# Ring tiles at multiples of 2048 bytes, and GpSimd's elementwise work on VectorE, in a hybrid decoder trunk

## The chip, the cores and the metric

One core of a Trainium2 chip runs the whole kernel. The metric is device microseconds of one execution; the runs shown give a median, and one further execution was profiled.

## The reference

One decoder layer on an input of 1024 tokens by 1024 channels, all in float32. The input is normalised, one wide projection (1024 x 10008) feeds four mixers, each mixer's result is projected back to 1024 channels, weighted by a sigmoid gate from the input, summed, passed through an output projection and added to the input. A SwiGLU feed-forward network and a final norm follow.

```python
xn = rmsnorm(h, norm_mix_w); proj = xn @ w_in
ya = hgrn2_branch(...); yb = ssd_branch(...); yc = gla_branch(...); yd = rglru_branch(...)
branch_out = einsum('blnw,nwd->blnd', stack([ya, yb, yc, yd]), w_branch)
merged = sum(sigmoid(mg) * branch_out, over the four)
h = h + merged @ w_out
xn = rmsnorm(h, norm_ffn_w)
h = h + (silu(xn @ w_gate) * (xn @ w_up)) @ w_ffn_out
return rmsnorm(h, norm_f_w)
```

The branch names: `ya` is HGRN2 and `yc` is GLA (both chunkwise gated linear attention), `yb` is the Mamba-2 SSD, `yd` is the RG-LRU.

## The kernel before, in words

**Split products.** A float32 product is made from three faster float32r matmuls. Every operand is split into a high part h (a rounded copy) and a low part l = raw - h, and the product is wh·ah + wh·al + wl·ah (`mm3`, L197 to 205; `mm3_tm`, L310 to 316; the feed-forward loops at L1105 to 1108 and L1201 to 1203). So each weight tile that arrives by DMA in `wr` costs a copy on ScalarE (L150) and a subtraction (L151). In the mixers `parts` (L148) does both, the subtraction on GpSimd (`G`). In the feed-forward network the same subtraction is written out on VectorE (`V`), at L1026, L1042, L1050, L1159 and L1168.

**Tiles.** All SBUF tiles of size come from one pool, `cp`. Rings of it are: `s` (26 slots of 128 x 1024), `wr`, `wh` and `wl` (two buffers each of 128 x 1024; raw weight, high, low), `t` (four of 128 x 512) and `x` (32 halves of 128 x 512, `half`). The pool gives a tag its place at the first tile taken of it, one behind the other, each tile padded to 32 bytes per partition. The pool begins 16512 bytes into a partition, 128 more than a multiple of 2048. Before the first slot come `prm0` (64 bytes), `prm` (448), `cst` (1536), `gtr` (1024) and `msk` (1024), 4096 in all. So the rings `s`, `wr` and `t` lie 128 bytes behind multiples of 2048. Then the 4-byte tiles `tiny` and `one` take 32 bytes each (L181 and L183), and `wh`, `wl` and `x`, whose first tiles are taken later, lie 192 bytes behind them. Operands of matmuls are columns of these tiles at multiples of 512 bytes, so an operand in `s` stands at 0 modulo 128 and one in `wh`, `wl` or `x` at 64.

**Stages.** In the order of time: load, norm and transposes into `x` halves (to about 40 us); RG-LRU (`conv` L403, gates L429, scans L458); then `merge(3)`; HGRN2 `attention` per head (L483), with the next head's projections between; `merge(0)`; GLA attention; the SSD's convolutions; `merge(2)` with one SSD `chunk` (L815) inside each of its steps; the SSD's gated norm (L892 to 915); eight gates, and the last branch (L930); the output projection (L1071); the feed-forward input (`ffn_in`) from about 1465 us and output (`tile_block`) from about 1895 us.

**`merge(b, y)`** (L390) runs over eight column tiles. Each step projects a gate (48 matmuls of 512 columns, `gate` L364) and a branch (24 matmuls, `branch` L376). VectorE multiplies gate and branch out of PSUM (L380), and the step adds into `merged` (L384, on GpSimd for three of the branches; the first has nothing to add to, the last one, at L930, is already on VectorE).

**What orders the work.** The tile framework orders the instructions of all engines ahead of time by priority and its own durations and puts in the semaphores; each engine then works through its own list in order. `tc.high_priority()` draws weight loads and their splits forward. DMAs of weights are issued by SyncE as the two `wr` buffers come free, that is after L150 and L151 have read them; L151 writes a `wl` buffer as soon as TensorE has done with the tile before the last (L205).

```python
def parts(h, l, raw):
    i = A.copy(h, raw)
    G.tensor_sub(l, raw, f32(h))
    return i
```

Of the kernel before, what the change touches and what calls it, by code (L numbers as in the profile page):

```python
# [30 lines left out]
F32 = mybir.dt.float32  # L31
F32R = mybir.dt.float32r
I32 = mybir.dt.int32
U8 = mybir.dt.uint8
# [4 lines left out]
P = 128  # L39
T = 1024  # L40
D = 1024
NT = T // P
KD = D // P
BW = 512
# [27 lines left out]
def trunk(ctx: ExitStack, tc: tile.TileContext, x, w_in, w_branch, w_out, w_fin, w_fout, prm_d, gw_d, lw_d,  # L72
          nfw_d, snw_d, cst_d, msk_d, out):
    nc = tc.nc
    V, A, G, TE = nc.vector, nc.scalar, nc.gpsimd, nc.tensor
    mult, add, sub, mx, mn = ALU.mult, ALU.add, ALU.subtract, ALU.max, ALU.min

    cp = ctx.enter_context(tc.tile_pool(name="cp", bufs=1))
# [37 lines left out]
    def f32(t):  # L116
        return t.bitcast(F32)
# [3 lines left out]
    prm = cp.tile([P, NPRM], F32, name="prm")  # L121
    cst = cp.tile([P, 3 * P], F32, name="cst")
    gtr = cp.tile([P, 2, P], F32R, name="gtr")
    msk = cp.tile([P, 2, 8, 64], U8, name="msk")

    ident, tri = cst[:, 0:P], (cst[:, P:2 * P], cst[:, 2 * P:3 * P])

# [20 lines left out]
    def parts(h, l, raw):  # L148

        i = A.copy(h, raw)  # L150
        G.tensor_sub(l, raw, f32(h))  # L151
        return i

    def load_w(src, nk, raw=None):
# [11 lines left out]
    for t in range(NT):  # L166
# [5 lines left out]
        if t % 4 == 3:  # L172
            c = C_LX + t // 4 * P
# [4 lines left out]
    nc.sync.dma_start(gt, cst_d[:, 3 * P:5 * P])  # L178
    mskf = slot()
    nc.sync.dma_start(mskf, msk_d)  # L180
    tiny = cp.tile([P, 1], F32, name="tiny")  # L181
    V.memset(tiny, 2.0 ** -115)
    one = cp.tile([P, 1], F32, name="one")  # L183
    V.memset(one, 1.0)

    def hs(hf):
        return slice(hf * H, (hf + 1) * H)
# [9 lines left out]
    def mm3(p, w, act):  # L197

        wh, wl = w
        n = len(act)  # L200
        for k, (ah, al) in enumerate(act):
            TE.matmul(p, lhsT=wh[k], rhs=ah, start=k == 0, stop=False)  # L202
            TE.matmul(p, lhsT=wh[k], rhs=al, start=False, stop=False)  # L203
        for k, (ah, al) in enumerate(act):
            TE.matmul(p, lhsT=wl[k], rhs=ah, start=False, stop=k == n - 1)  # L205

    def cut(w, nk, at=0):
        return [[a[:, k, at:at + P] for k in range(nk)] for a in w]
# [57 lines left out]
    for hf in range(2):  # L266
        norm_x(hf)
        if hf == 0:
            wlx.append(load_w(None, KD, rlx[0]))
        xn[hf] = split_fm(xt[hf * 4:hf * 4 + 4], "nmix", allbank)  # L270
        if hf == 0:
            wlx.append(load_w(None, KD, rlx[1]))
            for i in range(2):
                first[i] = dense_bank()
                mm3(first[i], cut(wlx[i], KD), xn[0])
    tc.keep_in_program_order(G.tensor_copy(gtr.rearrange("p a m -> p (a m)"), gt))
    tc.keep_in_program_order(G.tensor_copy(msk.rearrange("p a l m -> p (a l m)"), mskf))
    slot.free(mskf)
# [97 lines left out]
    def branch(b, dm, act, g, eng):  # L376

        ps = dense_fm(cut(wbr[b, dm // 2], 4, dm % 2 * P), act)
        for hf in range(2):
            V.scalar_tensor_tensor(g[:, hs(hf)], g[:, hs(hf)], 1.0, ps[hf], op0=add, op1=mult)  # L380
        if merged[dm] is None:
            merged[dm] = g
        else:
            eng.tensor_add(merged[dm], merged[dm], g)  # L384
            slot.free(g)

    def as_act(y):
        return [[(h[:, hs(hf)], l[:, hs(hf)]) for h, l in y] for hf in range(2)]

    def merge(b, y, also=None):  # L390

        for dm in range(KD):
            if also:
                also(dm)
            g = gate(b, dm)
            if dm % 2 == 0:
                load_br(b, dm)
            branch(b, dm, as_act(y), g, G)
        for h, l in y:
            slot.free(h, l)  # L400

# [51 lines left out]
    for i in range(4):  # L453
        j = A.activation(th[i], th[i], AF.Sqrt, bias=tiny)
# [5 lines left out]
    for i in range(4):  # L460
# [3 lines left out]
        g = act_slot(ps, AF.Gelu_apprx_tanh)  # L464
# [284 lines left out]
    NH = 8  # L749
# [31 lines left out]
    for ab in range(2):  # L781
# [4 lines left out]
            TE.matmul(pp, lhsT=gtr[:, ab, :], rhs=dahv[:, cols], start=True, stop=False)  # L786
            TE.matmul(pp, lhsT=gtr[:, ab, :], rhs=dalv[:, cols], start=False, stop=pp is after)
        TE.matmul(whole, lhsT=tri[ab], rhs=dav[:, cols], start=False, stop=True)
    ex = cp.tile([P, 3, NT, NH], F32, name="ex")
    A.activation(ex, p[:, 0:192].rearrange("p (i c h) -> p i c h", i=3, c=NT), AF.Exp)  # L790
    eg = cp.tile([P, NT, 4], F32, name="eg")
    V.tensor_copy(eg[0:64], ex[0:64, 2, :, 0:4])
    V.tensor_copy(eg[64:P], ex[64:P, 2, :, 4:8])
    bt = slot()
# [20 lines left out]
    def chunk(c):  # L815
        ab, at = c % 2, place(c)
        cs = slice(at * P, (at + 1) * P)
        xd = tmp()
        xdv = xd.rearrange("p (h q) -> p h q", h=NH)
        Xr = Xv[at // 2][:, at % 2, :]  # L820
        Xc = Xr.rearrange("p (h q) -> p h q", h=NH)
        V.tensor_tensor(xdv, Xc, dt[:, at, :].unsqueeze(2).broadcast_to(hb), op=mult)
        yp = sbank()
        for g in range(2):
            gs = slice(g * 64, (g + 1) * 64)
            cb = tbank()
            TE.matmul(cb[:, 0:P], lhsT=bt_f[gs, cs], rhs=ct[gs, cs], start=True, stop=True)
            cbm = cbm2()
            V.tensor_mul(cbm, cb[:, 0:P], tri[ab])

            lp = tbank()
            for i, part in enumerate((dah, dal)):
                td = tmp(F32R)
                V.tensor_tensor(quad(td), tri[ab].unsqueeze(1).broadcast_to([P, 4, P]),
                                  f32(part)[:, at, g * 4:(g + 1) * 4].unsqueeze(2).broadcast_to([P, 4, P]), op=mult)
                TE.matmul(lp, lhsT=gtr[:, ab, :], rhs=td, start=i == 0, stop=i == 1)
            dl = tmp()
            A.activation(dl, lp, AF.Exp)
            V.tensor_tensor(quad(dl), quad(dl), cbm.unsqueeze(1).broadcast_to([P, 4, P]), op=mult)
            for h in range(4):  # L840
                hh = g * 4 + h
                TE.matmul(yp[:, hh * 64:(hh + 1) * 64], lhsT=dl[:, h * P:(h + 1) * P], rhs=xdv[:, hh, :],
                          start=True, stop=True)
        V.tensor_tensor(Xc, Xc, pv("dsk", 0, 8).unsqueeze(2).broadcast_to(hb), op=mult)
        V.tensor_add(Xr, Xr, yp)
        if c:
            yt = tmp()
            for g in range(2):
                gs = slice(g * 64, (g + 1) * 64)
                yo = sbank()[:, 0:256]  # L850
                TE.matmul(yo, lhsT=ct[gs, cs], rhs=S[gs, c % 4, :], start=True, stop=True)
                V.tensor_tensor(yt[:, g * 256:(g + 1) * 256].rearrange("p (h q) -> p h q", h=4),
                                yo.rearrange("p (h q) -> p h q", h=4),
                                ex[:, 0, at, g * 4:(g + 1) * 4].unsqueeze(2).broadcast_to([P, 4, 64]), op=mult)
            G.tensor_add(Xr, Xr, yt)
        if c < NT - 1:
            V.tensor_tensor(xdv, xdv, ex[:, 1, at, :].unsqueeze(2).broadcast_to(hb), op=mult)
            up = tbank()
            for g in range(2):
                gs = slice(g * 64, (g + 1) * 64)  # L860
                TE.matmul(up[gs, 0:256], lhsT=btv[:, at, gs], rhs=xd[:, g * 256:(g + 1) * 256], start=True, stop=True)
            Sn = S[:, (c + 1) % 4, :]
            if c:
                V.tensor_tensor(Sn.rearrange("p (h q) -> p h q", h=4),
                                S[:, c % 4, :].rearrange("p (h q) -> p h q", h=4),
                                eg[:, at, :].unsqueeze(2).broadcast_to([P, 4, 64]), op=mult)
                V.tensor_add(Sn, Sn, up[:, 0:256])
            else:
                V.tensor_copy(Sn, up[:, 0:256])
# [14 lines left out]
    zz = [slot() for _ in range(4)]  # L884
# [7 lines left out]
    for c in range(NT):  # L892
        j, hf = c // 2, c // 4
        if c % 4 == 0:
            yb[hf] = [(slot(F32R), slot(F32R)) for _ in range(2)]
        Xr = Xv[j][:, c % 2, :]
        G.tensor_mul(Xr, Xr, zz[j][:, c % 2 * BW:(c % 2 + 1) * BW])
        sq = tmp()
        ss = sm.tile([P, 2], F32, name="ss2", tag="s2")
        for g in range(2):  # L900
            A.activation(sq[:, g * 256:(g + 1) * 256], Xr[:, g * 256:(g + 1) * 256], AF.Square, accum_out=ss[:, g:g + 1])
        r = rstd_of(ss, 2, 1.0 / 256)
        for g in range(2):
            gs = slice(g * 256, (g + 1) * 256)
            V.scalar_tensor_tensor(Xr[:, gs], Xr[:, gs], r[:, g:g + 1], snb[:, gs], op0=mult, op1=mult)
        p = tbank()
        for k in range(4):
            TE.transpose(p[:, k * P:(k + 1) * P], Xr[:, k * P:(k + 1) * P], ident)
        for kp in range(2):
            h, l = (a.rearrange("p (k t) -> p k t", k=2)[:, :, c % 4 * P:(c % 4 + 1) * P] for a in yb[hf][kp])  # L910
            pk = p[:, kp * 256:(kp + 1) * 256].rearrange("p (k t) -> p k t", k=2)
            A.copy(h, pk)
            V.tensor_sub(l, pk, f32(h))
        if c % 2:
            slot.free(X[j], zz[j])
# [11 lines left out]
    for dm in range(KD):  # L927
# [3 lines left out]
        for hf in range(2):  # L931
            h, l = half(F32R), half(F32R)
# [273 lines left out]
    for hf in range(2):  # L1206
# [11 lines left out]
        for t in range(4):  # L1218
            for j in range(NFF - LATE, NFF):
                tile_block(hf, t, j)  # L1220
            y, sq = slot(), slot()
# [81 lines left out]
```

## Time and profile before

| | us |
|---|---|
| median of 3 runs (2155.83 to 2160.21) | 2156.05 |
| the profiled execution, its own time | 2143.17 |
| span of the profiled execution | 2140.2 |
| TensorE busy | 2052.1 |
| VectorE busy | 974.3 |
| ScalarE busy | 634.0 |
| GpSimd busy | 328.1 |

In the profile PE is TensorE's matmuls, DVE is VectorE, ACT is ScalarE and POOL is GpSimd. L151 is line 151 of the kernel. A row's `[1.32 <-DVE t L834]` is the idle time of the engine ahead of the instruction and the instruction whose end released it. `pd<-x,wh` names the tiles that an instruction writes and reads, without buffer numbers; of a matmul's two operands one is the stationary (the weights held in the array, 128 columns) and one the moving one. Durations of matmuls overlap, so their pace is read from start to start. A granted clock of 1.00 is 2.4 GHz and 0.50 is 1.2 GHz.

### The profile page before, as it was taken

How to read it: one execution, taken by the hardware profiler on the slowest of the kernel's cores; microseconds unless marked ns; L12 is line 12 of the kernel's file. 1: busy time of each engine (PE TensorE's matmuls, PEld its weight loads, DVE VectorE, ACT ScalarE, POOL GpSimd, SP SyncE). 2: the span in 40 equal slices, each digit the busy share in tenths (PEclk: the TensorE clock that was granted, in tenths of full speed). 3: DMA queues.
4: the chain of work that ended last, by engine and by line, in shares of the span. 5: the costliest groups of instructions: out<-in, count | busy, mean ns of one | idle time of the engine just before them, and what ended most of it. 6: DMA issues, size and time to landing. Idle time of an engine off the chain costs nothing.

```text
span 2140.2 us, 24073 instructions
## 1 busy us (share of the span) xinstructions
PE 2052.1 (96%) x9892; PEld 1678.6 (78%) x9892; DVE 974.3 (46%) x1594; ACT 634.0 (30%) x943; POOL 328.1 (15%) x154
## 2 busy tenths in 40 slices
PE   6989999999999999989999899999999999999998
PEld 5679887889888777866668888776888888888886
DVE  6460005655110366556442504448666555554532
ACT  5652112332421121431112322235222222243321
POOL 2130122121133311113224223200000000000000
PEclk9999999999999999999999999999999999999999
DMA  5020111111111101111102011412322222266451
GB/s 164 24 62 24 49 50 40 27 45 31 31 50 40 50 21 29 32 40 30 30 30 70 6 50 59 148 60 68 109 85 65 86 89 89 99 207 220 144 166 40
DMA packets 157772, 147.56 MB, mean 69 GB/s; under 512 B 7472, under 2 KB 134880, under 8 KB 157664
## 3 DMA queue, kind: packets, MB, share of 16 engines
q1 hardware_dynamic: 153824, 136.82, 20.9%
q10 hardware_dynamic: 3840, 9.23, 1.1%
q8 instruction: 77, 1.26, 0.3%
q14 instruction: 31, 0.25, 0.0%
HBM read 126.10 MB, written 19.92 MB: 68 GB/s over the span
## 4 chain that ended last, share of the span: by engine, by line
PE 81%; DVE 11%; issue 4%; ACT 2%; DMA 1%; POOL 1%; SPq 0%; ACTq 0%; DVEq 0%; POOLq 0%
PE pd L203 12%; PE pd L202 12%; PE pd L205 11%; PE pd L1108 3%; PE pd L1106 3%; PE pd L1105 3%; PE pd L316 3%; PE pd L315 3%; PE pd L314 3%; PE pd L1202 2%; PE pd L1201 2%; PE pd L1203 2%; PE pq L1106 2%; PE pq L1108 2%; PE pq L1105 2%
## 5 line engine op out<-in xcount | busy, mean ns | idle before, releaser
L202 PE MATMUL pd<-x,wh 128*128 128x512 f32 x1056 | 427.2, 405 | 6.5 <-ACT s L346 6.0
L203 PE MATMUL pd<-x,wh 128*128 128x512 f32 x1056 | 423.5, 401 | 0.0
L151 POOL TENSOR_TENSOR wl<-wr,wh 128x1024 fp32r<-128x1024 f32 x82 | 200.9, 2450 | 815.9 <-PE pd L205 595.0
L205 PE MATMUL pd<-x,wl 128*128 128x512 f32 x1056 | 269.7, 393 | 0.0
L202 PEld LDWEIGHTS pd<-x,wh 128*128 128x128 f32 x1056 | 202.4, 192 | 52.4 <-ACT s L346 6.5
L203 PEld LDWEIGHTS pd<-x,wh 128*128 128x128 f32 x1056 | 202.3, 192 | 45.0 <-issue 6.1
L205 PEld LDWEIGHTS pd<-x,wl 128*128 128x128 f32 x1056 | 197.1, 188 | 42.9 <-issue 2.9
L380 DVE SCALAR_TENSOR_TENSOR s<-s,pd 128x512 f32<-128x512 f32 x64 | 43.9, 686 | 400.0 <-PE pd L205 400.0
L314 PE MATMUL pd<-s,x 128*128 128x256 f32 (+2 forms) x512 | 160.6, 314 | 2.9 <-ACT x L933 1.6
L316 PE MATMUL pd<-s,x 128*128 128x256 f32 (+2 forms) x512 | 161.0, 315 | 2.0 <-DVE x L934 2.0
L315 PE MATMUL pd<-s,x 128*128 128x256 f32 (+2 forms) x512 | 160.4, 313 | 0.9 <-POOL s L151 0.9
L150 ACT CAST wh<-wr 128x1024 fp32r<-128x1024 f32 x82 | 86.0, 1048 | 247.2 <-PE pd L203 203.3
L368 ACT ACTIVATE s<-pd 128x512 f32<-128x512 f32 x64 | 38.3, 599 | 237.9 <-PE pd L205 237.9
L314 PEld LDWEIGHTS pd<-s,x 128*128 128x128 f32 x512 | 97.5, 191 | 9.5 <-ACT x L933 2.1
L316 PEld LDWEIGHTS pd<-s,x 128*128 128x128 f32 x512 | 98.0, 191 | 8.2 <-DVE x L934 2.4
L315 PEld LDWEIGHTS pd<-s,x 128*128 128x128 f32 x512 | 97.4, 190 | 7.4 <-POOL s L151 1.4
L203 PE MATMUL pd<-s,wh 128*128 128x512 f32 x256 | 101.0, 394 | 0.0
L202 PE MATMUL pd<-s,wh 128*128 128x512 f32 x256 | 100.9, 394 | 0.0
L1159 DVE TENSOR_TENSOR s<-wr,s 128x1024 fp32r<-128x1024 f32 x44 | 53.9, 1225 | 73.2 <-ACT s L1158 53.4
L521 DVE COPY_PREDICATED s<-msk,pq 128x256 f32<-128x256 uint8 x128 | 62.1, 555 | 49.5 <-PE pq L508 27.6
L1025 ACT CAST wh<-wr 128x1024 fp32r<-128x1024 f32 x22 | 23.1, 1048 | 163.4 <-PE pq L1106 80.4
L205 PE MATMUL pd<-s,wl 128*128 128x512 f32 x256 | 70.3, 395 | 0.0
(343 smaller groups left out, 3753.8 us busy)
## 6 DMA issues: line engine op xcount, KB each, us to landing
wr<-in_w_in SPq DMA_DIRECT2D x76, 512.0 KB, 3.7
wr<-in_w_fin SPq DMA_DIRECT2D x44, 512.0 KB, 4.5
wr<-in_w_fout SPq DMA_DIRECT2D x44, 512.0 KB, 3.7
asp<-s SPq DMA_DIRECT2D x22, 512.0 KB, 4.9
x<-asp SPq DMA_DIRECT2D x42, 256.0 KB, 3.9
wr<-in_w_branch SPq DMA_DIRECT2D x16, 512.0 KB, 3.4
s<-in_x SPq DMA_DIRECT2D x8, 512.0 KB, 7.5
wr<-in_w_out SPq DMA_DIRECT2D x8, 512.0 KB, 3.7
```

The costliest lines, as they stand in the source:

```text
L150: i = A.copy(h, raw)
L151: G.tensor_sub(l, raw, f32(h))
L202: TE.matmul(p, lhsT=wh[k], rhs=ah, start=k == 0, stop=False)
L203: TE.matmul(p, lhsT=wh[k], rhs=al, start=False, stop=False)
L205: TE.matmul(p, lhsT=wl[k], rhs=ah, start=False, stop=k == n - 1)
L314: TE.matmul(p, lhsT=ah, rhs=wh, start=k == 0, stop=False)
L315: TE.matmul(p, lhsT=ah, rhs=wl, start=False, stop=False)
L316: TE.matmul(p, lhsT=al, rhs=wh, start=False, stop=k == n - 1)
L521: V.copy_predicated(dst[:, :, :, side, :], m, pv_[ab][:, i].rearrange("p c (n h) -> p c n h", h=h))
L1105: TE.matmul(p, lhsT=ah[:, k], rhs=bh, start=first and k == 0, stop=False, skip_group_check=True)
L1106: TE.matmul(p, lhsT=ah[:, k], rhs=bl, start=False, stop=False, skip_group_check=True)
L1108: TE.matmul(p, lhsT=al[:, k], rhs=bh, start=False, stop=k == KH - 1, skip_group_check=True)
```

## The change

The order in which tiles are taken from the pool changes: `ex` (768 bytes) and `eg` (128) are taken at the top in place of `msk` (1024), and `msk`, `tiny` and `one` are taken after the first tiles of `x`, `wh` and `wl`. The first 3968 bytes then end at 20480, ten times 2048, and all the rings begin at multiples of 2048. Five GpSimd instructions of the source are given to VectorE: the low part of `parts` (all the mixers' weights and w_out's), the adds of `merge`, and the SSD's add and product. GpSimd keeps its memsets (L490, L667, L694, L730) and the two casts at L276 and L277.

```diff
-    msk = cp.tile([P, 2, 8, 64], U8, name="msk")
+    ex = cp.tile([P, 3, NT, 8], F32, name="ex")
+    eg = cp.tile([P, NT, 4], F32, name="eg")
...
     def parts(h, l, raw):
         i = A.copy(h, raw)
-        G.tensor_sub(l, raw, f32(h))
+        V.tensor_sub(l, raw, f32(h))
...
-    tiny = cp.tile([P, 1], F32, name="tiny")
-    V.memset(tiny, 2.0 ** -115)
-    one = cp.tile([P, 1], F32, name="one")
-    V.memset(one, 1.0)
...
                 mm3(first[i], cut(wlx[i], KD), xn[0])
+    msk = cp.tile([P, 2, 8, 64], U8, name="msk")
+    tiny = cp.tile([P, 1], F32, name="tiny")
+    V.memset(tiny, 2.0 ** -115)
+    one = cp.tile([P, 1], F32, name="one")
+    V.memset(one, 1.0)
     tc.keep_in_program_order(G.tensor_copy(gtr.rearrange("p a m -> p (a m)"), gt))
...
-            branch(b, dm, as_act(y), g, G)
+            branch(b, dm, as_act(y), g, V)
...
-    ex = cp.tile([P, 3, NT, NH], F32, name="ex")
...
-    eg = cp.tile([P, NT, 4], F32, name="eg")
...
-            G.tensor_add(Xr, Xr, yt)
+            V.tensor_add(Xr, Xr, yt)
...
-        G.tensor_mul(Xr, Xr, zz[j][:, c % 2 * BW:(c % 2 + 1) * BW])
+        V.tensor_mul(Xr, Xr, zz[j][:, c % 2 * BW:(c % 2 + 1) * BW])
```

## Rows read from the trace of the kernel before

**Rows 1.** The page, engines: busy us, share of the span, instructions.

```profile
PE 2052.1 (96%) x9892; PEld 1678.6 (78%) x9892; DVE 974.3 (46%) x1594; ACT 634.0 (30%) x943; POOL 328.1 (15%) x154
```

**Rows 2.** Waits of PE: line, releaser: us in total, times, longest us.

```profile
PE pt L353 <- ACT s L772: 6.9, 4, 1.8
PE pt L908 <- DVE s L913: 6.8, 1, 6.8
PE pq L429 <- DVE s L410: 6.2, 2, 3.6
PE pq L596 <- DVE s L605: 6.2, 2, 3.8
...
PE pt L836 <- DVE t L834: 6.0, 6, 1.3
PE pq L515 <- DVE s L542: 5.4, 2, 4.5
PE pq L842 <- DVE t L839: 5.2, 3, 1.7
```

**Rows 3.** Groups by line, POOL: count | busy us, mean ns | idle before, releasers.

```profile
L151 POOL TENSOR_TENSOR wl<-wr,wh 128x1024 fp32r<-128x1024 f32 x82 | 200.9, 2450 | 815.9 <-PE pd L205 595.0 <-ACT wh L150 164.2 <-ACT s L567 17.4
L151 POOL TENSOR_TENSOR s<-wr,s 128x1024 fp32r<-128x1024 f32 (+2 forms) x21 | 50.6, 2420 | 103.3 <-ACT s L150 91.6 <-PE pd L203 11.0 <-issue 0.7
L384 POOL TENSOR_TENSOR s<-s 128x1024 f32<-128x1024 f32 x16 | 39.5, 2466 | 32.8 <-DVE s L380 32.8
...
L897 POOL TENSOR_TENSOR s<-s 128x512 f32<-128x512 f32 x8 | 10.7, 1353 | 26.5 <-ACT s L887 26.5
```

**Rows 4.** Groups by line and form, DVE, same columns.

```profile
L834 DVE TENSOR_TENSOR t<-cst,dah 128x512 fp32r<-128x512 f32 x16 | 28.7, 1794 | 0.2 <-PE pt L836 0.2
...
L1026 DVE TENSOR_TENSOR wl<-wr,wh 128x1024 fp32r<-128x1024 f32 x22 | 26.9, 1225 | 16.6 <-ACT wh L1025 16.5
...
L408 DVE TENSOR_SCALAR s<-s,prm 128x1024 f32<-128x1024 f32 x10 | 17.2, 1725 | 35.9 <-ACT s L406 35.9
...
L834 DVE TENSOR_TENSOR t<-cst,dal 128x512 fp32r<-128x512 f32 x16 | 10.9, 680 | 0.1
```

**Rows 5.** Timeline, PE, a gate, its branch, the next gate: start us, us, instruction.

```profile
233.54 0.39 PE L202 MATMUL pd<-x,wh 128*128 128x512 f32 x1
...
238.98 0.39 PE L202 MATMUL pd<-s,wh 128*128 128x512 f32 x1
...
244.58 0.39 PE L202 MATMUL pd<-x,wh 128*128 128x512 f32 x1
```

**Rows 6.** Timeline, PE, two stretches of the feed-forward network: input, then output.

```profile
1701.47 0.39 PE L1105 MATMUL pd<-s 128*128 128x512 f32 x1
...
1704.19 0.39 PE L1105 MATMUL pd<-x,wh 128*128 128x512 f32 x1
...
1902.88 0.39 PE L1203 MATMUL pd<-s,x 128*128 128x512 f32 x1
...
1906.38 0.40 PE L1203 MATMUL pq<-s,x 128*128 128x512 f32 x1
```

**Rows 7.** Timeline of DVE, then of POOL, in one SSD chunk.

```profile
976.42 2.87 DVE L834 TENSOR_TENSOR t<-cst,dah 128x512 fp32r<-128x512 f32 x1
...
976.38 2.36 POOL L384 TENSOR_TENSOR s<-s 128x1024 f32<-128x1024 f32 x1 [5.60 <-DVE s L380]
```

**Rows 8.** Two stretches: us, busy us (x instructions) by engine, PEclk, DMA share, GB/s.

```profile
1006.80:1017.00 10.20, 10.20 (x28) 6.81 (x27) 5.04 (x8) 0.60 (x1) 1.66 (x1) 0.50 0.00 0
1017.00:1027.20 10.20, 10.20 (x47) 7.84 (x46) 1.95 (x4) 2.25 (x3) 2.07 (x1) 1.00 0.01 2
```

**Rows 9.** Timeline of DVE, an unheld L408.

```profile
63.80 0.81 DVE L408 TENSOR_SCALAR s<-s,prm 128x1024 f32<-128x1024 f32 x1 [2.85 <-ACT s L406]
```

**Rows 10.** Timeline of POOL, then of DVE, in a step of the first merge.

```profile
239.28 2.39 POOL L151 TENSOR_TENSOR wl<-wr,wh 128x1024 fp32r<-128x1024 f32 x1 [14.11 <-PE pd L205]
...
242.05 0.69 DVE L380 SCALAR_TENSOR_TENSOR s<-s,pd 128x512 f32<-128x512 f32 x1 [13.01 <-PE pd L205]
```

## The prediction

> **What bounds the kernel now.** I read the engines' totals first. TensorE is busy in 96% of the span, VectorE in 46% [rows 1]. So there are only two places to gain: the 88 us in which TensorE has nothing to do, and the pace of the matmuls themselves. GpSimd's 328 us cost nothing by themselves.
>
> The second view is TensorE's list of waits [rows 2]. Nearly all of it is for VectorE, directly or through ScalarE: the RG-LRU's convolutions (L429, 6.2 us), the ends and starts of attention (L596 and L515, 6.2 and 5.4), the SSD's convolutions (L353, 6.9, where the transposes wait for a ScalarE step behind them), the chunks (L836 and L842, 11.2 together) and the SSD's gated norm (L908, 6.8).
>
> Why is VectorE late, at 46%? Its groups kept apart by form show it: L834 is run on two tiles of one shape, and one takes 680 ns, the other 1794 in the mean [rows 4]. One instance of the slow one takes 2.87 us and lies beside GpSimd's add of the merge, which starts 0.04 us earlier and ends within 0.6 us of it [rows 7]. So a VectorE instruction that meets a GpSimd one is held until that is done. L408 is the same: 0.81 us alone, 1.73 in the mean of ten [rows 9, 4].
>
> The third view is the timeline of TensorE where it never waits. A gate's 24 matmuls (both operands at 64 modulo 128) take 5.44 us, 226.7 ns each; the 24 of the branch behind it (moving operand in `s` at 0, weights in `wh` or `wl` at 64) take 5.60 us, 233.3 ns each [rows 5]. In the feed-forward network 12 matmuls with both operands in `s` take 2.72 us, 226.7 each, and the output's 15 (moving operand in `s`, stationary one in `x`) take 3.50, 233.3 each [rows 6]. Equal phase 226.7, unequal phase 233.3, whichever the phase.
>
> **The change part by part.**
>
> *Places.* All rings come to phase 0, which both operands in `s` have already. So I take 226.7 for all. The unequal ones, counted in the code: the four branches 4 x 8 x 24 = 768, the output projection 2 x 8 x 24 = 384, the feed-forward output 1056 less the 48 of its first two blocks, 1008. Together 2160 x 6.6 ns = 14.3 us, all in stretches where TensorE works without a break. In the feed-forward input, 528 more have the moving operand in `x` and weights in `s`; no row prices them, and I bound them by 0 and 6.6 ns, 0 to 3.5 us, and take 2. The 256-column projections are also unequal; bound by 0 and half of 6.6 for some 960 of them, 0 to 3.2, taken as 0. Sum: -16 us, bounds 0 (if phase is not the cause) and -21.
>
> The Trainium skill ("TensorE: Matmul & The Clock Gate", Step-by-step: what each phase is for) speaks against this: TensorE reads moving operand and weights through two independent ports, and a weight load takes no bandwidth from a running matmul. By it the relative place of the two could not matter, this term would be 0 and the time below 2127 in place of 2111. The rows differ by 6.6 ns and go with the phase, so I go by them.
>
> *The subtractions.* 82 and 21 of L151, at 2450 and 2420 ns on GpSimd [rows 3], become VectorE's. L1026 is the same instruction on VectorE: 1225 ns [rows 4]. That adds 103 x 1.22 = 126 us to VectorE, the 16 adds of the merge 20, the seven adds and eight products of 512 columns 15 x 0.69 = 10: 156 us, against the holds that go. VectorE comes to about half of the span, far from a bound. What counts is what it does next to TensorE's waits. There a hold of up to 2.4 us is replaced by 1.22 us of work that is ahead in the same queue, so each held place gives back about 1.2 us:
> - Chunks. Even ones: L834 at 2.87 becomes 1.22 + 0.68, 0.97 less, three times. Odd ones have two holds, L834 by a subtraction (0.3 less by the same working, since it is caught late) and L839 by the add (0.95 less), three times. Sum 6.7 of the 11.2 us [rows 2].
> - SSD convolutions: L408 is held for about 1.5 us (17.2 us for ten, less ten times 0.81, over the six held ones); the subtraction starts some 0.5 us ahead of it and delays it by 0.7. Four waits x 0.85 = 3.4.
> - L429, two waits, 2.4. L596, two waits and a third that the list puts down to another line, 1.1 each, 3.3. L515, where two GpSimd instructions stand together, 2.4. L908: eight products go from 1353 to about 690 ns, but take the place of the holds that they cause; 1.5. Sum 9.6.
>
> Together -19.7 us. The last merge and the output projection, where eight subtractions (9.8 us) enter a VectorE that is dense, and the RG-LRU's scans I take as +1 (bounds -3 and +5): what hides the subtractions there is VectorE's slack, and where it is gone TensorE waits for L934.
>
> *The clock.* Behind the double wait of each odd chunk the granted clock is 0.50 for some 10 us: 28 matmuls where the next 10.2 us hold 47 [rows 8]. Three such stretches cost 5.1 us each. The two waits there are 1.7 us (L842, 5.2 by three) and 0.7 (L836, 6.0 less three of 1.3, by three) [rows 2]. After the change they are about 0.8 and 0.4, together less than the even chunks' single wait of 1.3, which no such stretch follows. I take two of the three back, -10; bounds 0 and -25, as other short stretches follow other waits.
>
> *Work that costs nothing.* The merges' adds (L384) and subtractions lie in TensorE-bound steps of 16.4 us: a subtraction that starts at 239.28 would end at 240.5, before the L380 at 242.05 for which VectorE had waited 13 us [rows 10]. `tiny`, `one` and `msk` are moved past nothing that waits for them early. No DMA moves; those of `wr` are issued earlier by the 1.2 us that a subtraction is shorter, wherever SyncE waits for L151. Where that is on the path, the bound is a gain of 2 us; I take 0.
>
> *Sum.* -16 - 19.7 + 1 - 10 = about -45 us. The profiled execution took 2143.2, so it would take 2098. The median of the runs is 2156.05, 0.6% above the profiled one; the same 45 us give 2111.
>
> **The rivals.**
>
> *A, the queue blocks: slower.* GpSimd waited 595 us for TensorE to be done with a `wl` buffer [rows 3], and nothing stood behind it. On VectorE everything stands behind it. In a merge step, if the subtraction is put ahead of the two L380 of the step before, these come only when the gate's last matmul has freed `wl`; the branch's banks are then late by 1.22 + 2 x 0.69 = 2.6 us in each of 24 steps: +62, with -45 a time of 2173. It decides from 1.9 us per step on. Against it: in the trace the subtraction starts 2.8 us before L380 [rows 10], and the tool orders by its own durations. The Trainium skill ("TensorE: Matmul & The Clock Gate", Architectural detail) says that VectorE's queue is strictly first in, first out, which is what A needs; no row here tests it by itself.
>
> *B, phase alone works.* VectorE's own new work fills what the holds leave, and the clock stretches stay: -16, 2140.
>
> *C, holds alone work.* The 6.6 ns come from something other than the phase (which ring is read, say), or the pool places tiles otherwise than I add up: -29, 2127.
>
> *D, neither:* the holds are replaced one for one and the pace stays: 2156.
>
> *E, every matmul gains.* If a 2048-byte boundary inside the moving operand costs another step of 6.6 ns in all the 7200 matmuls of 512 columns, -48 more: 2063. Against it: 226.7 appears at both phases, and nothing in the trace lies at 0 modulo 2048. The Trainium skill ("TensorE: Matmul & The Clock Gate", Back-to-back issue gap) gives N/2.4 + 2.5, 216 ns for 512 columns; by that alone all of them would gain 11 ns, and no row shows such a pace.
>
> **How the numbers follow.** Forecast 55%, B 15%, C 15%, A 7%, D 4%, E 4%. The likeliest time is 2111. The range takes in the forecast's own bounds (full phase, clock and wait terms: about -75, 2081) and B and C up to 2140: 2082 to 2142, which leaves out A, D and E. Faster by over 0.2% (some 4 us, about what a measurement of this kernel can tell from no change): forecast, B, C, E, 0.89. D is the same, 0.04. Slower is A, 0.07.
>
> **What would show it.** In the profile after: branch, output projection and feed-forward output at 226.7 ns from start to start, as the gates; if not, C (or E, if the gates change too). POOL down to memsets and two casts, some 20 us. L834 on its first tile and L408 at 0.68 and 0.81 us. TensorE's waits at L836 and L842 near 4.5 us in all, at L353 near 3.5. Granted clock 1.00 behind the odd chunks. VectorE's busy time near 974 + 156 less about 70 of holds. The forecast is wrong if TensorE shows waits for L380, or VectorE waits for PE L205 with a convolution or an attention step behind it.

## The result, and the profile after

| | before | after |
|---|---|---|
| median, us | 2155.94 (4 runs, 2146.71 to 2160.21) | 2052.40 (4 runs, 2050.95 to 2053.54) |
| profiled execution, its own time | 2143.17 | 2052.34 |
| its span | 2140.2 | 2050.4 |
| mean granted clock | 0.981 | 0.997 |

The ratio is 0.9525, with a 95% interval of 0.9493 to 0.9556: 103.5 us less by the medians, 90.8 by the two profiled executions. The prediction was 2111.0, with a range of 2082 to 2142. The direction was right; the time lies 30 us below the range.

The lines below carry the number of the changed kernel: from L151 to L205 they shift by one to three either way (L205 is L202, L202 is L199, L151's subtraction is L152), from L314 to L772 by two upward; from L829 on they are unchanged. The page's engines, as [rows 1]:

```profile
PE 2006.1 (98%) x9892; PEld 1663.1 (81%) x9892; DVE 1030.5 (50%) x1728; ACT 632.9 (31%) x942; POOL 14.2 (1%) x20
```

TensorE lost 46.0 us of busy time and 43.8 us of idle time (88.1 before, 44.3 now). The second view is TensorE's waits, as [rows 2]: line, releaser, us in total, times, longest.

```profile
PE pt L231 <- DVE s L259: 12.8, 1, 12.8
PE pd L199 <- ACT s L348: 7.0, 2, 5.3
...
PE pt L908 <- DVE s L913: 1.6, 1, 1.6
PE pq L517 <- DVE s L544: 1.3, 2, 0.7
...
PE pt L355 <- ACT s L774: 0.6, 3, 0.2
...
PE pq L431 <- DVE s L412: 0.5, 1, 0.5
...
PE pq L598 <- DVE s L607: 0.4, 1, 0.4
```

The waits of [rows 2] are nearly all gone: 6.9 became 0.6 (L355), 6.8 became 1.6 (L908), 6.2 became 0.5 (L431), 6.2 became 0.4 (L598), 5.4 became 1.3 (L517), and L836 and L842 have no row any more. What is left on top, L231 in the norm at the start and L199 in the RG-LRU, was there before at 12.7 and 6.0.

The third view is VectorE's groups by form, as [rows 3, 4]: count, busy us, mean ns, idle before and releasers.

```profile
L152 DVE TENSOR_TENSOR wl<-wr,wh 128x1024 fp32r<-128x1024 f32 x82 | 100.4, 1224 | 370.8 <-PE pd L202 264.4 <-ACT wh L151 103.3 <-ACT s L569 1.7
...
L834 DVE TENSOR_TENSOR t<-cst,dal 128x512 fp32r<-128x512 f32 x16 | 11.0, 685 | 0.0
L834 DVE TENSOR_TENSOR t<-cst,dah 128x512 fp32r<-128x512 f32 x16 | 10.9, 684 | 0.0
...
L410 DVE TENSOR_SCALAR s<-s,prm 128x1024 f32<-128x1024 f32 x10 | 8.1, 808 | 2.9 <-ACT s L408 2.9
```

L834 on its first tile went from a mean of 1794 ns to 684, the 680 of its second tile; L408, now L410, from 1725 to 808. The subtraction takes 1224 ns in place of 2450. And VectorE, whose queue now holds it, stands in front of it for 264.4 us until TensorE has done with a `wl` buffer.

The chunks, as [rows 7], by VectorE's timeline in one merge step of the changed kernel (start us, us, instruction):

```profile
931.03 1.23 DVE L152 TENSOR_TENSOR wl<-wr,wh 128x1024 fp32r<-128x1024 f32 x1
932.56 0.69 DVE L845 TENSOR_TENSOR s<-s,pq 128x512 f32<-128x512 f32 x1 [0.31 <-PE pq L842]
...
933.77 0.69 DVE L834 TENSOR_TENSOR t<-cst,dah 128x512 fp32r<-128x512 f32 x1
...
939.15 1.22 DVE L386 TENSOR_TENSOR s<-s 128x1024 f32<-128x1024 f32 x1
...
940.89 0.68 DVE L834 TENSOR_TENSOR t<-cst,dah 128x512 fp32r<-128x512 f32 x1
...
943.92 0.42 DVE L852 TENSOR_TENSOR t<-pq,ex 128x256 f32<-128x256 f32 x1 [1.55 <-PE pt L836]
```

The subtraction at 931.03 is over before the L845 behind it could start, which still waits 0.31 us for TensorE. The merge's add (L386) stands in the queue between the chunk's instructions, and the L834 behind it still comes in time: VectorE waits for TensorE's L836 afterwards, and not the other way round.

The two stretches of [rows 8] (us; busy us and instructions of PE, PEld, DVE, ACT, POOL; granted clock; DMA share; GB/s), which in this kernel are chunks again:

```profile
1006.80:1017.00 10.20, 10.20 (x50) 7.51 (x49) 7.27 (x13) 1.20 (x2) 0.00 (x0) 1.00 0.20 53
1017.00:1027.20 10.20, 10.20 (x47) 7.85 (x46) 5.91 (x10) 2.25 (x3) 0.00 (x0) 1.00 0.06 20
```

TensorE's timeline, as [rows 5, 6]: the first two rows are the start of a branch's 24 matmuls and of the gate behind them; from the third to the fourth are 32 matmuls of the feed-forward output, stationary operand in `x`:

```profile
231.32 0.39 PE L199 MATMUL pd<-s,wh 128*128 128x512 f32 x1
...
236.76 0.39 PE L199 MATMUL pd<-x,wh 128*128 128x512 f32 x1
...
1814.25 0.39 PE L1203 MATMUL pd<-s,x 128*128 128x512 f32 x1
...
1821.50 0.39 PE L1202 MATMUL pt<-s,x 128*128 128x512 f32 x1
```

5.44 us by 24 and 7.25 by 32 are both 226.7 ns. The branch took 5.60.

**Where the 90 us went.** To split TensorE's time I took the intervals from each matmul's start to the next, all 9892 of them, less a base (226.7 ns for 512 columns, which is the equal-phase pace, half of it for 256, and a tenth percentile of each shape for the rest; the level of the waits depends on this choice, their differences do not). Excess in stretches at granted clock 0.50 is "half clock"; of the others, excess above 20 ns is a wait, below it is pace. The last half-clock stretch of each kernel runs on past the span's end. The same for every run that follows, in us:

| kernel | waits | half clock | pace of 512 columns | pace of 256 | half-clock stretches |
|---|---|---|---|---|---|
| before | 176.0 | 42.7 | 18.9 | 0.4 | 14, 85.0 us |
| after | 139.0 | 2.7 | 1.8 | 4.6 | 2, 12.9 |
| places alone | 171.5 | 54.8 | 1.4 | 5.0 | 13, 104.3 |
| engines alone | 138.0 | 1.9 | 19.3 | 0.4 | 2, 15.0 |
| holds put back | 176.1 | 11.1 | 2.0 | 4.6 | 6, 29.7 |
| subtractions alone | 144.7 | 15.0 | 1.5 | 4.6 | 5, 39.0 |
| adds and products alone | 162.1 | 23.4 | 1.8 | 4.6 | 9, 52.3 |
| all at 128 | 136.7 | 4.4 | 1.9 | 4.6 | 3, 15.9 |
| `x`, `wh`, `wl` at 32 | 137.4 | 3.9 | 22.4 | 3.1 | 3, 18.2 |
| no low parts | 144.8 | 22.8 | 1.4 | 4.8 | 6, 49.5 |
| square on ScalarE | 138.4 | 2.2 | 1.8 | 4.6 | 2, 14.1 |

Before to after: waits -37.0, half clock -40.0, pace of 512 columns -17.1, of 256 columns +4.2, together -89.9 of the 89.8 us by which the span shrank. Another 13 us of the medians' difference lies in runs of before that were not profiled: the median is 12.8 us above the profiled execution, that of after 0.1. They too go with the clock. Of the 13 runs of before that stand beside places alone, the five at 2143 to 2146 us have a mean granted clock of 0.980 or 0.981, as the profiled one, and the eight from 2154.8 up have 0.971 to 0.975.

### The profile page after: what moved, and what is told of

It is laid out like the page before. It is cut to its first block, busy times and chain, and to the rows that moved or that the text cites. A ratio compares the mean times of both kernels' runs of the same rounds, so it can differ in the third digit from the quotient of the medians.

```text
span 2050.4 us, 23991 instructions
## 1 busy us (share of the span) xinstructions
PE 2006.1 (98%) x9892; PEld 1663.1 (81%) x9892; DVE 1030.5 (50%) x1728; ACT 632.9 (31%) x942; POOL 14.2 (1%) x20
## 4 chain that ended last, share of the span: by engine, by line
PE 89%; DVE 7%; ACT 2%; issue 1%; DMA 1%; SPq 0%; DVEq 0%; ACTq 0%
PE pd L199 13%; PE pd L200 13%; PE pd L202 13%; PE pd L1106 3%; PE pd L1105 3%; PE pd L1108 3%; PE pd L318 3%; PE pd L316 3%; PE pd L317 3%; PE pd L1202 2%; PE pd L1203 2%; PE pd L1201 2%; PE pq L1108 2%; PE pq L1106 2%; PE pq L1105 2%; PE pt L1105 1%
## 5 line engine op out<-in xcount | busy, mean ns | idle before, releaser
L199 PE MATMUL pd<-x,wh 128*128 128x512 f32 x1056 | 420.1, 398 | 7.4 <-ACT s L348 7.0
L200 PE MATMUL pd<-x,wh 128*128 128x512 f32 x1056 | 418.1, 396 | 0.0
L152 DVE TENSOR_TENSOR wl<-wr,wh 128x1024 fp32r<-128x1024 f32 x82 | 100.4, 1224 | 370.8 <-PE pd L202 264.4
L202 PE MATMUL pd<-x,wl 128*128 128x512 f32 x1056 | 271.9, 394 | 0.0
L199 PEld LDWEIGHTS pd<-x,wh 128*128 128x128 f32 x1056 | 199.4, 189 | 51.8 <-ACT s L348 7.8
L200 PEld LDWEIGHTS pd<-x,wh 128*128 128x128 f32 x1056 | 199.4, 189 | 41.1 <-issue 2.4
L202 PEld LDWEIGHTS pd<-x,wl 128*128 128x128 f32 x1056 | 196.4, 188 | 42.8 <-issue 3.5
L151 ACT CAST wh<-wr 128x1024 fp32r<-128x1024 f32 x82 | 86.3, 1052 | 249.5 <-PE pd L200 227.8
L199 PE MATMUL pd<-s,wh 128*128 128x512 f32 x256 | 99.8, 390 | 0.0
L200 PE MATMUL pd<-s,wh 128*128 128x512 f32 x256 | 99.8, 390 | 0.0
L382 DVE SCALAR_TENSOR_TENSOR s<-s,pd 128x512 f32<-128x512 f32 x64 | 43.9, 687 | 94.5 <-PE pd L202 94.5
L202 PE MATMUL pd<-s,wl 128*128 128x512 f32 x256 | 68.5, 389 | 0.0
```

The lines of the kernel that those rows point to most:

```text
L152: V.tensor_sub(l, raw, f32(h))
```

## The experiments

The kernel before was run beside every group of these; its medians there were 2154.93, 2145.71 and 2155.26. All but "engines alone" and "no low parts" are told as edits of the changed kernel. The "five instructions" of the section on the change and of the expectations are four in the source: the low part of `parts`, the merge's add, and the SSD's add and product. The low part, L151, makes two of the five groups of GpSimd's rows that went.

### The two halves of the change

Places alone: the changed kernel with these instructions back on GpSimd.

```diff
-        V.tensor_sub(l, raw, f32(h))
+        G.tensor_sub(l, raw, f32(h))
...
-            branch(b, dm, as_act(y), g, V)
+            branch(b, dm, as_act(y), g, G)
...
-            V.tensor_add(Xr, Xr, yt)
+            G.tensor_add(Xr, Xr, yt)
...
-        V.tensor_mul(Xr, Xr, zz[j][:, c % 2 * BW:(c % 2 + 1) * BW])
+        G.tensor_mul(Xr, Xr, zz[j][:, c % 2 * BW:(c % 2 + 1) * BW])
```

> The kernel after with its five instructions given back to GpSimd: only the places of the tiles change, and every engine's list of instructions is that of the kernel before. Phase theory: the 2160 matmuls of unequal phase go from 233.3 to 226.7 ns, the 256-column ones lose some 4 us (120 in place of 113 to 118 ns), so 10 to 16 us less than before; the waits of TensorE and the stretches at a granted clock of 0.50 stay, about 140 us of the span and 0.98 mean clock. Rival (the clock follows the pace or the places): mean granted clock 0.99 or more and 40 to 60 us less. Rival (places do nothing): within 4 us of before.

Engines alone: the kernel before with them on VectorE, its places untouched.

> The kernel before with the five instructions on VectorE and the tiles where they were: every engine's list is that of the kernel after. Hold theory: the waits and the half-clock stretches go as in the kernel after (mean clock 0.995 or more), so 75 to 90 us less than before, and 10 to 16 us more than after. Rival (the clock follows the places): clock near 0.98 and 35 to 45 us less than before.

Places alone took 2138.54 us, ratio 0.9930 (0.9906 to 0.9954), 16 us less than before. Engines alone took 2065.48, ratio 0.9601 (0.9567 to 0.9634), 89 us less. Together that is 105, and the whole change brought 103.5, so the halves add up. Each half has, in its trace, the lists of the kernel that it was meant to have: in places alone all engines' instructions stand in the order of before, in engines alone in that of after. The phase shows in engines alone on TensorE's timeline: a branch, and the gate behind it.

```profile
228.81 0.39 PE L202 MATMUL pd<-s,wh 128*128 128x512 f32 x1
...
234.41 0.39 PE L202 MATMUL pd<-x,wh 128*128 128x512 f32 x1
```

5.60 us again, 233.3 ns each. In places alone the pace term is 1.4 in place of 18.9, while waits hardly fall (171.5, before 176.0) and half clock does not (54.8, before 42.7): the gain of the phase is not one of the clock.

### Which of the instructions

Subtractions alone on VectorE (of the four edits above the last three), then adds and products alone (of the four the first).

> The kernel after with the merges' adds and the SSD's add and product back on GpSimd: only the 103 subtractions are on VectorE. Hold theory: the chunks' waits return in part (L834 and L839 beside the merge's add, about 2 us each, eight or so), with their half-clock stretches: 10 to 35 us more than after. If the subtractions' holds are all that matters: within 5 us of after.

> The kernel after with the 103 subtractions back on GpSimd; the merges' adds and the SSD's add and product stay on VectorE. Hold theory: the chunks lose the holds of L834 and L839 by the add and keep those by the subtractions; convolutions (L355, 6.9 us), attention (L517, L598) and their half-clock stretches wait as before: 25 to 60 us more than after. If the adds made the gain: within 20 us of after.

Subtractions alone took 2069.85 us, adds and products alone 2094.91. Against places alone that is -68.7 and -43.6, together more than the -86.1 of both. Most of the overlap is half clock: against places alone 39.8 and 31.4 us of it go, together 71.2, and with both only 52.1. And they share chunks: with one of them left on GpSimd, L836 or L842 still waits. VectorE's timeline in subtractions alone:

```profile
961.90 1.22 DVE L152 TENSOR_TENSOR wl<-wr,wh 128x1024 fp32r<-128x1024 f32 x1
...
963.24 2.67 DVE L834 TENSOR_TENSOR t<-cst,dah 128x512 fp32r<-128x512 f32 x1
```

and GpSimd's there:

```profile
962.06 3.29 POOL L386 TENSOR_TENSOR s<-s 128x1024 f32<-128x1024 f32 x1 [13.36 <-DVE s L382]
```

The add comes 0.16 us after the subtraction has begun on VectorE and takes 3.29 us in place of 2.47; L834 comes behind the subtraction, beside the add, and takes 2.67 in place of 0.68. Each held the other here. TensorE's waits in this kernel:

```profile
PE pt L908 <- DVE s L913: 5.7, 1, 5.7
PE pt L836 <- DVE t L834: 5.7, 5, 1.3
PE pq L517 <- DVE s L544: 1.4, 2, 0.7
...
PE pq L842 <- DVE t L839: 1.1, 1, 1.1
PE pt L355 <- ACT s L774: 0.6, 3, 0.2
...
PE pq L431 <- DVE s L412: 0.5, 1, 0.5
```

and with adds and products alone:

```profile
PE pt L355 <- ACT s L774: 6.9, 4, 1.8
PE pq L431 <- DVE s L412: 6.2, 2, 3.6
...
PE pq L598 <- DVE s L607: 5.9, 2, 3.6
PE pq L517 <- DVE s L544: 3.5, 2, 2.5
...
PE pq L842 <- DVE t L839: 1.9, 3, 0.6
PE pt L908 <- DVE s L913: 1.6, 1, 1.6
```

In subtractions alone L598 has 0.4. So L355, L431, L598 and most of L517 belonged to the subtractions, L908 to the product, L836 to the adds, and L842 to both. The Trainium skill ("SBUF — State Buffer", Who interferes with whom) says the same of two-input instructions as L834: a VectorE instruction with two inputs in SBUF and a GpSimd one that reads SBUF exclude each other for a whole instruction, and the one issued first has it. The 2.67 and the 3.29 us agree.

### Is it the hold, or the order of the lists?

Moving an instruction also changes the order that the framework gives every list. Two kernels change the holds and leave the order nearly as it is. Of TensorE's 9892 instructions 9880 stand in the same order in holds put back as in the changed kernel, and 9891 in no low parts as in places alone; of VectorE's, 1695 of 1728 and 1590 of 1594. Holds put back: the changed kernel, and behind each subtraction on VectorE a GpSimd one whose result nobody reads.

```diff
         V.tensor_sub(l, raw, f32(h))
+        G.tensor_sub(raw, raw, f32(h))
         return i
```

> The kernel after, plus a GpSimd subtraction on each raw weight tile behind VectorE's, in place and read by nobody: the work stays on VectorE and GpSimd holds it up again. Hold theory: VectorE's L834-like instructions beside GpSimd take over 1.5 us again, TensorE's waits and half-clock stretches return in part: 30 to 80 us more than after. Rival (the shorter subtraction or the new order of the lists made the gain, not the end of the holds): within 10 us of after.

No low parts: places alone, with a GpSimd memset in place of the subtraction, which reads nothing.

```diff
-        G.tensor_sub(l, raw, f32(h))
+        G.memset(f32(l), 0.0)
```

> The mixers' and the output projection's weight low parts are left out: GpSimd writes zeros in their place (a memset, some 0.95 us, no SBUF operand read) and VectorE does none of it; the adds and the SSD's add and product stay on GpSimd. The lists of TensorE, VectorE and ScalarE are nearly those of the kernel before, the places those of after. If the holds themselves made TensorE's waits: as the run with the subtractions alone on VectorE, 2065 to 2080 us. If the new order of the lists made the gain: 2120 to 2140 us, as with the places alone.

Holds put back took 2102.95 us, 50 more than the changed kernel, and the sum of its waits came back to 176.1, that of before. L835 (L834, one line on) is held again, four of 32 at 2.61 to 2.68 us and the others at 0.68 or 0.69. But part of the sum may be not the hold itself: the extra instruction also keeps a `wr` buffer longer. Its list:

```profile
PE pd L200 <- ACT s L349: 9.1, 2, 7.4
PE pt L356 <- ACT s L775: 8.6, 4, 2.2
...
PE pt L837 <- DVE t L835: 3.7, 4, 1.0
```

L356 and L837 (L355 and L836) stop TensorE again, 8.6 and 3.7 us where before had 6.9 and 6.0, though VectorE has all the work. L200, in the RG-LRU, waits longer in total than in any other kernel (9.1 us), so the equal sum is not made of the same waits.

No low parts took 2078.14, 60 less than places alone: waits fell from 171.5 to 144.8 us, half clock from 54.8 to 22.8, L410's mean from 1726 to 887 ns. The lists are nearly the same, and TensorE's list in places alone has only 0.9 us of waits for the subtraction itself, so the holds made the difference and not the memset's shorter time. This kernel, which has no subtraction anywhere, stands at 144.8 us of waits beside 144.7 for subtractions alone, which has all 103 in VectorE's queue (adds and products on GpSimd in both). But the two equal sums are made of unequal rows. No low parts:

```profile
PE pq L842 <- DVE t L839: 3.4, 3, 1.1
PE pd L199 <- ACT s L348: 3.2, 1, 3.2
PE pq L598 <- DVE s L607: 3.1, 2, 2.3
...
PE pq L431 <- DVE s L412: 0.8, 2, 0.6
...
PE pt L355 <- ACT s L774: 0.7, 3, 0.2
```

Subtractions alone has 0.5 at L431 and 0.6 at L355: there the new work on VectorE cost TensorE nothing. At L199, the end of the RG-LRU's chain, it has 6.9, 3.7 more; one subtraction of 1.22 us stands in VectorE's chain there, the rest is not traced. At L842 and L598 it has less, 1.1 and 0.4, and for L598 the timelines of GpSimd and VectorE in no low parts show why:

```profile
759.14 1.89 POOL L492 MEMSET s<- 128x1024 f32 x2
759.26 0.88 DVE L217 TENSOR_SCALAR r<-v 128x8 int32<-128x8 int32 x1
```

L217 takes 0.17 us in subtractions alone. So GpSimd's memsets, which read nothing, hold some VectorE instructions too, and no low parts is not quite free of holds. That all the subtractions together cost TensorE nothing is therefore not shown.

### Which property of the place counts

All at 128: a pad of 128 bytes ahead of the rings, so that all begin 128 bytes behind a multiple of 2048.

```diff
     eg = cp.tile([P, NT, 4], F32, name="eg")
+    pad = cp.tile([P, 32], F32, name="pad")
+    V.memset(pad, 0.0)
```

> The kernel after with a pad of 128 bytes ahead of the rings, so that all of them lie 128 bytes behind multiples of 2048; the engines' lists are the same but for one small memset. Phase theory (only the two operands' relative place counts): within 2 us of after, 226.7 ns for 512 columns, 120 for 256. Rival (it is the multiple of 2048 that counts): 10 to 16 us more than after.

`x`, `wh` and `wl` at 32: a pad of 32 bytes behind the first tiles of `s` and `t`.

```diff
     gt = tmp()[:, 0:2 * P]
+    pad = cp.tile([P, 8], F32, name="pad")
+    V.memset(pad, 0.0)
```

> The kernel after with a pad of 32 bytes behind s, wr and t, so that wh, wl and x lie 32 bytes behind multiples of 2048 and s at them. Phase theory with any difference counting: the matmuls between s and wh, wl or x pace at 233 ns again, the 256-column ones below 120, 10 to 14 us more than after. If only a difference of 64 counts: within 3 us of after.

All at 128 took 2051.48 us, the same as the change: the multiple of 2048 does nothing, the common phase does it. At 32 it took 2070.97, 18.6 more than the change and above the 10 to 14 expected: even `x` moving with `s` stationary paces at 233.4 ns there, and the 256 columns gain little. Operands lie at multiples of 512 bytes in their tiles, so the differences tested are 0 modulo 512, 32 and 64 bytes. That 128 is the period is not tested. In the kernel at 32 TensorE's timeline has a branch and the gate behind it 5.60 us apart, as at 64:

```profile
230.55 0.40 PE L201 MATMUL pd<-s,wh 128*128 128x512 f32 x1
...
236.15 0.39 PE L201 MATMUL pd<-x,wh 128*128 128x512 f32 x1
```

### A candidate to beat both

The longest wait left in the middle is 5.3 us for L348, behind VectorE's chain in the RG-LRU. One product of that chain goes to ScalarE.

```diff
-        V.tensor_mul(a2, rr[i], rr[i])
+        A.activation(a2, rr[i], AF.Square)
```

> The changed kernel with one instruction moved: the RG-LRU's square of the gate (V.tensor_mul of rr[i] by itself) becomes a ScalarE activation (Square). The longest wait left to TensorE after the change is 5.3 us for ScalarE's L348, at the end of a chain of VectorE instructions of which this product is one, and a stretch of 6.8 us at half clock follows it. Theory (VectorE's chain ends last there): the wait gets shorter by about one VectorE instruction of 1024 columns, 1.2 us, in each place, and the half-clock stretch behind it may go, so 3 to 8 us less than the changed kernel, 2044 to 2049. Rival (ScalarE is as full there, since the square stands in its queue ahead of the exponentials): within 2 us of 2052. Second rival: the square on ScalarE pushes back L348 itself, and the time is longer, 2054 to 2060.

> The changed kernel itself, unaltered, on the chip of the run before it, as the measure for that run: 2050 to 2054. If it is outside of this, the difference between the two is to be read from this call alone.

The square on ScalarE took 2053.06 us, the changed kernel beside it 2051.86: within the first rival's 2 us, no difference that can be measured. In the changed kernel, ScalarE ahead of the L348 that ends the 5.3 us wait:

```profile
121.11 1.04 ACT L360 CAST s<-s 128x1024 fp32r<-128x1024 f32 x1 [9.48 <-DVE s L468]
122.06 1.08 ACT L348 ACTIVATE s<-pd 128x512 f32<-128x512 f32 x2
```

ScalarE stood idle for 9.48 us, until VectorE's chain of products and scans had come to L468: the theory had the right chain for this wait. With the square added, VectorE's and ScalarE's timelines:

```profile
103.34 1.22 DVE L459 TENSOR_TENSOR s<-s 128x1024 f32<-128x1024 f32 x1 [3.14 <-ACT s L456]
...
109.63 1.09 ACT L348 ACTIVATE s<-pd 128x512 f32<-128x512 f32 x2
```

VectorE now waits 3.14 us for ScalarE's L456, which has the squares among the work ahead of it, and the chain ends less than 1 us earlier. TensorE's two waits of 1.7 and 5.3 us for L348 became one of 7.6. Nothing tried beats the change.

## Why the prediction was wrong

**Places: right, 16 predicted.** The medians give 16 for places alone; the trace gives 17.5 for 512 columns, and 4.6 back for 256, 12.9 together. The mechanism was right, with two terms mis-sized. The 528 feed-forward inputs with `x` moving and `s` stationary ran at 229.8 ns before and 226.7 now, 1.6 us where 2 was taken. The 256-column projections, bounded by a gain of 0 to 3.2, lost: 115.4 ns in the mean of 960 before, 119.9 now. That bound assumed that every size wants the same phase, with no row for it. Rival E, that all matmuls gain, is out: the gates stay at 226.7. The Trainium skill ("TensorE: Matmul & The Clock Gate", Step-by-step: what each phase is for) states two independent read ports, as the prediction said. What the prediction drew from that, that this term would be 0, is contradicted by places alone.

**Holds: the step that failed.** It reads: "a hold of up to 2.4 us is replaced by 1.22 us of work that is ahead in the same queue, so each held place gives back about 1.2 us". The places it prices had 45.0 us of waits in TensorE's list before ([rows 2], and 2.3 for L596 behind L521: L353 6.9, L908 6.8, L429 6.2, L596 6.2 and 2.3, L836 6.0, L515 5.4, L842 5.2). The step left 25.3 of them; 4.4 are left. Nearly the whole hold came back, 40.6 us by TensorE's list and 37.0 by intervals (which set waits inside half-clock stretches apart), against 19.7. On GpSimd the subtraction ran whenever a `wl` buffer came free, and held whatever VectorE had next. On VectorE it is one more entry in an ordered list, and in this list it stands where nobody is late: ahead of L845 at 931.03, in the rows above, where L845 had to wait for TensorE anyway and the next L834 is still in time. The step took the place in time of the GpSimd instruction for the new one's place in the queue. At L431 and L355 no low parts beside subtractions alone shows that the replacement cost nothing; at L199 it may have cost some of the 3.7 us by which the two differ. That the framework's priorities put it there is read from one timeline and not tested.

**Clock: the second, larger miss.** I took 10 us back, two of the chunks' three stretches, with a bound of 25. It was 40.0: 85.0 us at half clock in 14 stretches became 12.9 in 2. The three in the chunks were 30.6 of the 85.0; the prediction priced only these and left the others to its bound. Places alone (54.8) and engines alone (1.9) show that it belongs to the engines' half. But the sum of waits doesn't set it: holds put back has the waits of before, 176.1, and 11.1 us; no low parts and subtractions alone have equal waits, and 22.8 and 15.0. Which wait is followed by such a stretch is left open.

The last step of the sum failed with it. It carried the 0.6% between the profiled execution and the median over to the new time, as if it were no part of the gain. These 12.8 us became 0.1. As the runs' granted clocks go, they were half clock as well, so that by the medians the clock's term was some 53 us (an estimate, 40.0 and 12.7).

**The rest.** The last merge and the scans, +1: TensorE's list has no wait for L382, and the 2.0 us that the list of before has for L934 are gone; behind the RG-LRU's scans the wait for L348 grew from 6.0 to 7.0. VectorE's busy time was put near 974 + 156 - 70 = 1060; it is 1030.5, so the holds had taken about 100 us of it. GpSimd: 14.2, as foreseen some 20.

**Rival A** had its mechanism and not its price: the queue does stand in front of the subtraction, 264.4 us for L202, and VectorE's timeline in the first merge shows what follows.

```profile
231.58 1.23 DVE L152 TENSOR_TENSOR wl<-wr,wh 128x1024 fp32r<-128x1024 f32 x1 [10.18 <-PE pd L202]
234.24 0.69 DVE L382 SCALAR_TENSOR_TENSOR s<-s,pd 128x512 f32<-128x512 f32 x1 [1.44 <-PE pd L202]
```

The L382 behind it waits another 1.44 us for TensorE: the buffer comes free before the products are there. B and C each deny one half, D both, and both halves worked.

The range failed with the same two terms. Its lower end, 75 us less, had 21 for places and 25 for the clock, which leaves some 29 for waits. The profiled executions gave 12.9, 40.0 and 37.0, and the medians another 12.7. Holds and clock were short together, and engines alone shows that both came from the engines' half.

## What to carry to other kernels

When a VectorE instruction is slow only sometimes, look for a GpSimd instruction that begins beside it; moving that work to VectorE can cost little (here 156 us of it; no row of TensorE's waits grew by more than 1.2 us), if TensorE's waits are nearly all for held instructions. Price the removal of a wait at its whole size as the gain's bound, and ask of every wait that goes whether a half-clock stretch follows it, since that was worth as much again. Place a matmul's two operands without a difference of 32 or 64 bytes between their addresses (0 modulo 512 was right here, others are not tested), and time each column count by itself.

## What was not expected of the hardware

The 256-column matmuls ran at 115.4 ns with operands 64 bytes apart, at 118.3 with 32, and at 119.9 at equal phase, the opposite of the 512-column ones (233.3, 233.3, 226.8). And with 512 columns it matters which operand is moved: `x` moving at 64 with `s` stationary at 0 ran at 229.8, `s` moving with `x` stationary at 233.3; with `x` at 32 both took 233.3 or 233.4. The paces are means over all such matmuls of a trace without those that waited or ran at half clock. And a GpSimd memset, which has no input in SBUF, held a VectorE instruction on eight columns for 0.88 us in place of 0.17.
